# Stage work dealt out by column counts during attention, and one relu moved behind a copy, in a one-layer encoder block

## The chip, the cores and the metric

The kernel runs on one core of a Trainium2 chip. The metric is the device time of one execution in microseconds. TensorE is the matrix engine (PE in the profile), VectorE is DVE, ScalarE is ACT, GpSimd is POOL, and SyncE (SP) issues most of the transfers. Each engine works through its own queue in order; semaphores tie the queues together.

## The reference, cut to what matters

One encoder layer on 1024 tokens of width 1024:

```
u = rms_norm(x, g1)
q, k, v, cb, cc, ch, ga, gb = split(u @ w_in)
y_a = neighbourhood_attention(rms_norm(q), rms_norm(k), v, rpb) @ w_attn_branch   # 8 heads x 64
y_b = (cb * conv3(cc * ch, conv_w)) @ w_conv_branch                               # 512 channels
x = x + (sigmoid(ga) * y_a + sigmoid(gb) * y_b) @ w_o
h = rms_norm(x, g2) @ w_mlp_in                                                    # 4096 wide
x = x + relu(h)^2 @ w_mlp_out
```

The attention window is 8 rows by 16 columns on a 16 x 64 grid, with a learned bias by relative position. Everything is float32 at input and output.

## The kernel before, in words

Each float32 operand is cut into a high and a low 16-bit part, and a product is the sum of three matmuls (`PASSES`). ScalarE makes the high part (a scaled copy), VectorE the low part (scale, then subtract the high part). This holds for weights (`Chunk.prep`, high part L284, low part L276) and for results. Before the parts of a chunk of weights are cut, its scale is found, from sums of squares (ScalarE, L241) or from maxima (VectorE, L295), then a small matmul with a column of ones (L179) and a few VectorE instructions on one column.

The program is written as one stream of issues. Preparations are Python generators in two lists: `fg` holds work that follows from results, `bg` the preparation of weights. `step` and `tick` advance them, and each `yield` in a generator ends what one advance issues. A generator that cannot go on yet yields `WAIT`. So the order on every engine is fixed when the program is built.

**Attention** (about 168 to 327 us). There are 64 steps (4 head pairs, 8 blocks, 2 heads), and a loop of `N + 15` rounds over `k` in which each step's work is spread over 15 rounds: scores (`at_qk`, L785, two matmuls into one of three "s" banks), bias and row maximum on VectorE (`at_max`, L799), exponential on ScalarE (`at_exp`, L808), reciprocals (L812, L813), high part (`at_hi`, ScalarE L821), low part (`at_lo`, VectorE L825), transposition by a transfer on SP (L830), weighted sums of V (`at_pv`, L842), and, when a bank is full, its copy to the high and low part of the result (`at_out`, ScalarE L854 and VectorE L855, in one round). Between these TensorE is given the products of the short convolution (`conv_mms`, L861), seven or eight a round. These need the weights of four convolution chunks; while one chunk is used, the next is prepared from `bg`. When a chunk comes up that is not yet ready, `flush` forces it out.

In the same rounds `conv_step` advances the convolution itself, one chunk at a time: `conv_post` (product of two banks, L687, L691, and the gating product L699), `conv_taps` (the three taps, L705, L708, and GpSimd L710, L713) and `conv_split` (square L720, scale, high part L729, low part L733). The preparation from `bg` gets one `tick` a round, and a second one in rounds in which no parts of weights were cut (`splitting`).

**First MLP product** (about 640 to 930 us). Sixteen groups `q` of columns, each a seven-product scheme (`seven`) on quarter matrices, in `quad`. The seven results are combined through a buffer `AS[q]`, of which there are two, or for the third group (`q == 2`) partly through two spare tiles. ScalarE copies the first bank (L1493), VectorE adds the others (L1474 to L1495). `h_done`, called from `post3` at the end of a group, then does relu (L1439) and square (L1441) on ScalarE, four sums (L1161), and a store to memory (L1452). `post3` of a group runs while the next group's products are already issued. Its arguments `wait1` and `wait2` hold back relu and the sums by so many steps. Meanwhile the weights two groups on are scaled (L954), summed (L963, L968, L934, L935, L179) and cut (L983, L979).

Of the kernel before, what the change touches and what calls it, by code (L numbers as in the profile page):

```python
# [15 lines left out]
OP = mybir.AluOpType  # L16
# [36 lines left out]
def encoder_block(ctx: ExitStack, tc: tile.TileContext, x, weights, cols, gqk, rel, masks, out):  # L53
# [79 lines left out]
    def tick(n=1):  # L133

        for _ in range(n):
            i = 0
            while i < len(bg):
# [5 lines left out]
                else:  # L143
                    break

    def drain():
        while fg:
            step()
# [5 lines left out]
            step()  # L154
        forced[0] = False

    late, units, forced, side, splitting = [], [0], [False], [False], [False]
    work = [0]

    def apart(mark, n=3, of=units):  # L160
# [59 lines left out]
    class Chunk:  # L220
# [9 lines left out]
        def prep(self):  # L230
            n = len(self.widths)
            nk = sum(k for k, _ in self.widths)
            rm, a, b, s = (cols_of("prep", i) for i in (nk, 1, 1, 1))
            self.inv = keep()
            tot = sum(k * w for k, w in self.widths)
            if self.kind in "QKCG" or self.half:
                self.parts = vhome[0][:, 1] if self.half else wsp.tile([128, 2, tot], F16, name="w16_ws", tag="ws")
                for p, (k, w) in enumerate(self.widths):
                    while len(self.raw) <= p:
                        yield WAIT  # L240
                    A.activation(self.parts[:, 1, :k * w].bitcast(BF16), self.raw[p][:, :k * w], AF.Square,  # L241
                                 accum_out=sc[:, at(rm, p)])
                    yield
                V.tensor_reduce(sc[:, a], sc[:, at(rm, 0, n)], axis=AX, op=OP.add)
                c = ones_col()
                V.tensor_tensor(c, sc[:, a], sc[:, gm2], op=OP.mult)
                if not self.half:
                    yield from apart(units[0], 2 if self.kind == "Q" else 3)
                yield from all_sum(c, b, bank(self.bank) if self.bank else anybank(), 1e-36, not self.half)
                yield from pow2_half(b, 14, s, self.inv, more=self.more)  # L250
            else:
                yield from self.largest(rm, a, b)
                yield from pow2(b, 14, s, self.inv, False, more=self.more)
            V.tensor_scalar(sc[:, rm], sc[:, self.rows], sc[:, s], None, op0=OP.mult)  # L254
            yield
            while done[0] < self.first or self.tag not in wpool:
                yield WAIT
            if self.half is not None:
                if not self.half:
                    vhome.append(wsp.tile([128, 2, 2, tot], F16, name="w16_v", tag="ws"))  # L260
                self.parts = vhome[0][:, self.half]
            elif self.kind not in "QKCG":
                self.parts = wpool[self.tag].tile([128, 2, tot], F16, name="w16_" + self.tag, tag=self.tag)
            f = o = 0
            todo = []
            for p, (k, w) in enumerate(self.widths):
                todo.append((p, [(i * w, w, rm.start + o + i) for i in range(k)], f))
                f += k * w
                o += k
            prev = None  # L270
            for it in todo + [None]:
                if prev:
                    p, parts, f = prev
                    for o, m, c in parts:
                        hi, lo = (self.parts[:, w, f + o:f + o + m] for w in range(2))
                        V.scalar_tensor_tensor(lo, self.raw[p][:, o:o + m], sc[:, c:c + 1], hi,  # L276
                                               op0=OP.mult, op1=OP.subtract)
                    done[0] += 1
                    load_upto(done[0] + 5)
                splitting[0] = True  # L280
                if it:
                    p, parts, f = it
                    for o, m, c in parts:
                        A.activation(self.parts[:, 0, f + o:f + o + m], self.raw[p][:, o:o + m], AF.Copy,  # L284
                                     scale=sc[:, c:c + 1])
                prev = it
                self.split = it is None
                yield

        def largest(self, rm, a, b):  # L290
            o = 0
            for p, (k, w) in enumerate(self.widths):
                while len(self.raw) <= p:
                    yield WAIT
                V.tensor_reduce(sc[:, at(rm, o, k)], self.raw[p][:, :k * w].rearrange("p (k w) -> p k w", k=k),  # L295
                                axis=AX, op=OP.max, apply_absolute_value=True)
                o += k
                yield
            while not self.ready:
                yield WAIT  # L300
            mul(rm, self.rows, rm)
            yield
            V.tensor_reduce(sc[:, a], sc[:, rm], axis=AX, op=OP.max, apply_absolute_value=True)
            c = ones_col()
            V.tensor_copy(c, sc[:, a])
            if self.kind != "V":
                yield from apart(units[0], 3 if self.kind != "O" else 1 + (self is cO[1]))
            yield from all_sum(c, b, bank(self.bank) if self.bank else anybank(), 1e-30, self.kind != "V")
# [369 lines left out]
    def conv_post(j, g, half, ps, d):  # L678
# [3 lines left out]
        if g == 0:  # L682
            if half == 0:
                d["z"] = w2p.tile([128, S + 2], F32, name="z", bufs=1)
                G.memset(d["z"][:, 0:1], 0.0)
                G.memset(d["z"][:, S + 1:S + 2], 0.0)
            A.activation(perm(d["z"][:, 1:S + 1], half), p3, AF.Copy, scale=sc[:, ch.inv])  # L687
            return
        if g == 1:
            zn = perm(d["z"][:, 1:S + 1], half)  # L690
            V.tensor_tensor(zn, p3, zn, op=OP.mult)  # L691
            if half == 1:
                d["cv"] = w2p.tile([128, S], F32, name="cv", bufs=1)
                conv_tail.append(conv_taps(ch, d))
            return
        while not d.get("taps"):
            yield
        cv = d["cv"]
        V.tensor_tensor(perm(cv, half), p3, perm(cv, half), op=OP.mult)  # L699
        if half == 1:  # L700
            conv_tail.append(conv_split(j, cv))

    def conv_taps(ch, d):
        z, cv, c = d["z"], d["cv"], ch.cwj
        A.activation(cv, z[:, 0:S], AF.Copy, scale=sc[:, at(c, 0)])  # L705
        yield
        yield
        V.scalar_tensor_tensor(cv, z[:, 1:S + 1], sc[:, at(c, 1)], cv, op0=OP.mult, op1=OP.add)  # L708
        yield
        G.tensor_scalar(z[:, 2:], z[:, 2:], sc[:, at(c, 2)], 1.0, op0=OP.mult, op1=OP.mult)  # L710
        yield
        for c in range(0, S, 256):
            G.tensor_tensor(cv[:, c:c + 256], cv[:, c:c + 256], z[:, c + 2:c + 258], op=OP.add)  # L713
        yield
        d["taps"] = True

    def conv_split(j, cv):
        ch = cConv[j]
        m, s, inv = tmp(), tmp(), tmp()
        A.activation(BT[:, 1, j].bitcast(BF16), cv, AF.Square, accum_out=sc[:, m])  # L720
        yield
        V.tensor_scalar(sc[:, m], sc[:, m], 1e-36, None, op0=OP.max)
        yield
# [1 line left out]
        mul(inv, ch.inv, at(rowsB, j))  # L725
        G.tensor_scalar(cv, cv, sc[:, s], 1.0, op0=OP.mult, op1=OP.mult)
        yield
        bh, bl = (BT[:, w, j].rearrange("p (b r c) -> p b r c", b=8, r=16) for w in range(2))
        A.activation(bh, perm(cv), AF.Copy)  # L729
        yield  # L730
        pv = perm(cv)
        for b in range(0, 8, 2):
# [25 lines left out]
        V.tensor_scalar(sc[:, at(rowsA, k)], sc[:, cV[k // 2].inv], 2.0 ** 20, None, op0=OP.mult)  # L758
    for ch in cA:
        ch.ready = True  # L760

    def conv_step(n):

# [81 lines left out]
        for e in range(2):  # L845
            del st[s + e]

    def at_out(s):
        p, i, _ = steps[s]
        if i % 4 == 3:  # L850
            O = obank[p, i // 4]
            half = slice((i // 4) * 512, (i // 4 + 1) * 512)
            hi, lo_ = QD[:, p, 0, 0, half], QD[:, p, 0, 1, half]
            A.activation(hi, O, AF.Copy, scale=2.0 ** -14)  # L854
            V.scalar_tensor_tensor(lo_, O, 2.0 ** -14, hi, op0=OP.mult, op1=OP.subtract)  # L855

    conv = conv_mms(first)

# [1 line left out]
        for ps, l, r, a, b in islice(conv, n):  # L860
            T.matmul(ps, l, r, start=a, stop=b)  # L861

    for k in range(N + 15):
        p, w = k // 16, k % 16
        if p < 3 and w == 3:
            bias[p + 1] = bias_load(p + 1)
        if p < 3 and w in (9, 11):
            bias_make(*bias[p + 1], (w - 9) // 2)
        ok = lambda d: 0 <= k - d < N
        if ok(0):  # L870
            at_qk(k)
        emit(4)
# [11 lines left out]
            at_exp(k - 1)  # L884
        units[0] += 1
        conv_step(1)
        splitting[0] = False
        tick(1)
        if not splitting[0]:
            tick(1)  # L890
        emit(4 if k % 8 == 0 else 3)
        if k % 2 == 1 and ok(11):
            at_pv(k - 11)
        if k % 2 == 0 and ok(14):
            at_out(k - 14)
    emit(1000)
    while conv_live or conv_tail or conv_q:
        conv_step(1)
    for ch in cB:
        ch.ready = True  # L900
# [560 lines left out]
    def quad(q, c0=0, c1=512):  # L1461
# [24 lines left out]
        def post3(ps):  # L1486
# [1 line left out]
            if q == 0:  # L1488
                fg.append(h_done(q, c0, c1, 3, 4 if c0 else 24))
            elif c1 == 512:  # L1490
                fg.append(h_done(q, 0, c1, *((2, 6) if q == 1 else ())))
        seven(P1[q], actU2, c0, c1, {
            1: lambda ps: A.activation(z[4], ps[1], AF.Copy),  # L1493
            6: post6, 5: None if c0 else post5,
# [262 lines left out]
```

## Time and profile before

| | us |
|---|---|
| median of three executions | 1235.99 |
| lowest, highest | 1235.72, 1236.13 |
| profiled execution, its own time | 1236.98 |
| span of the profiled execution | 1235.0 |

The span is the time from the first to the last instruction on the core; 1.98 us of the profiled execution's time lie around it. In the profile's rows a line number is that of the kernel before. A row of the view of lines names the line, engine, operation, output and inputs, shapes and count, then busy us and the mean ns of one, then idle time ahead of the group and what ended it. A row of the timeline has the start, the time it took, and in square brackets the idle time ahead of it with what ended it. A row of the view of waits has the total in us, the count, and the longest. In a row of the view by stretches the columns are the stretch, its length, the busy time of TensorE, its weight loads, VectorE, ScalarE and GpSimd, then the granted TensorE clock, the share of the transfer engines, and GB/s.

### The profile page before, as it was taken

The numbers are of one execution on the slowest core, as the hardware profiler recorded it, in microseconds if no ns is written. First come the engines' busy times: TensorE is split into PE (matmuls) and PEld (weight loads), VectorE is DVE, ScalarE is ACT, GpSimd is POOL, SyncE is SP. The second block draws the span as 40 slices with busy tenths as digits, with TensorE's granted clock in tenths as the row PEclk, the third lists the DMA queues.
The fourth block names the chain that finished last, engine by engine and source line by source line (L and its number), as shares of the span: only waits on it lengthen the run. The fifth ranks groups of instructions, "written<-read, shape, count | busy, mean of one in ns | idle before, by whom it ended". The sixth has DMA issues, their size and how long they took to land.

```text
span 1235.0 us, 17055 instructions
## 1 busy us (share of the span) xinstructions
PE 1198.7 (97%) x6294; PEld 574.6 (47%) x6294; DVE 932.7 (76%) x1754; ACT 768.2 (62%) x1186; POOL 422.5 (34%) x273
## 2 busy tenths in 40 slices
PE   4999998999999999999999999999999999999998
PEld 3544444444444444444458444444444444444444
DVE  6667877888557686887888664555547999998997
ACT  6785777787464454536668777777765763646430
POOL 0440003112231111101003466655648373463562
PEclk9999999999999999999999999999999999999999
DMA  6548555756561211216096544554484844435202
GB/s 261 117 185 171 109 114 120 154 122 103 131 142 43 68 52 51 69 35 256 18 181 155 193 149 152 169 186 138 146 289 162 307 162 161 175 113 217 102 35 103
DMA packets 170867, 173.35 MB, mean 140 GB/s; under 512 B 131488, under 2 KB 132000, under 8 KB 166688
## 3 DMA queue, kind: packets, MB, share of 16 engines
q1 hardware_dynamic: 170208, 168.07, 46.5%
q10 hardware_dynamic: 576, 4.19, 0.9%
q8 instruction: 49, 0.80, 0.3%
q14 instruction: 34, 0.28, 0.1%
HBM read 102.51 MB, written 37.75 MB: 114 GB/s over the span
## 4 chain that ended last, share of the span: by engine, by line
PE 61%; DVE 22%; ACT 9%; issue 5%; DMA 3%; SPq 0%; ACTq 0%; DVEq 0%
PE ps_d L188 23%; PE ps_s L188 20%; PE ps_o L188 15%; PE ps_d L861 3%; DVE sz L799 2%; DVE P L825 2%; DVE w_s L979 2%; DVE w_ws L276 1%; ACT w_ws L241 1%; DVE ops L1590 1%; DMA qD<-q 1%; DVE w L979 1%; DVE u L416 1%; DVE s L480 1%; DVE sg L1095 1%
## 5 line engine op out<-in xcount | busy, mean ns | idle before, releaser
L188 PEld LDWEIGHTS <-ops 128*128 128x128 f16 x1356 | 132.4, 98 | 159.4 <-issue 2.4
L188 PEld LDWEIGHTS <-w 128*128 128x128 f16 x1368 | 133.2, 98 | 144.7 <-issue 5.9
L861 PE MATMUL ps_d<-uT,w_ws 128*128 128x512 f16 x528 | 125.4, 379 | 0.0
L188 PE MATMUL ps_d<-ops 128*128 128x512 f16 (+1 forms) x528 | 118.3, 374 | 0.0
L188 PE MATMUL ps_s<-ops 128*128 128x512 f16 x492 | 113.2, 379 | 1.6 <-DVE ops L1590 1.1
L1581 ACT ACTIVATE ops<-hf,sc 128x2048 f16<-128x2048 f32 x26 | 52.0, 2000 | 95.3 <-PE ps_o L188 35.9
L188 PEld LDWEIGHTS <-uT 128*128 128x128 f16 x648 | 64.7, 100 | 69.0 <-issue 4.3
L968 POOL TENSOR_TENSOR tsum<-raw 128x512 f32<-128x512 f32 x28 | 45.7, 1646 | 146.0 <-ACT raw L954 146.0
L1161 POOL TENSOR_TENSOR as<-as 128x512 f32<-128x512 f32 x56 | 76.7, 1370 | 44.4 <-ACT as L1441 41.1
L188 PEld LDWEIGHTS <-w_s 128*128 128x128 f16 x588 | 56.7, 98 | 69.5 <-DVE w_s L979 2.0
L188 PE MATMUL ps_d<-u2x,w 128*128 128x512 f16 (+1 forms) x360 | 80.0, 372 | 0.0
L188 PE MATMUL ps_o<-ops 128*128 128x512 f16 x336 | 77.1, 379 | 0.0
L1583 DVE SCALAR_TENSOR_TENSOR ops<-hf,sc,ops 128x2048 f16<-128x2048 f32 x26 | 72.2, 2776 | 5.2 <-ACT ops L1581 5.2
L861 PEld LDWEIGHTS <-w_ws 128*128 128x128 f16 x528 | 50.8, 98 | 52.5
L188 PE MATMUL ps_o<-u2T,w 128*128 128x512 f16 (+1 forms) x324 | 73.4, 377 | 0.0
L954 ACT ACTIVATE raw<-raw,sc 128x256 f32<-128x256 f32 x172 | 71.0, 496 | 1.1 <-DMA raw<-in_weights 1.1
L968 POOL TENSOR_TENSOR gsum<-raw 128x512 f32<-128x512 f32 x14 | 19.0, 1374 | 131.7 <-ACT raw L954 55.3
L983 ACT ACTIVATE w<-raw,sc 128x512 f16<-128x512 f32 (+1 forms) x28 | 24.7, 929 | 49.8 <-DVE sc L404 49.8
L808 ACT ACTIVATE sz<-sz,sc 128x384 f32<-128x384 f32 (+1 forms) x64 | 37.4, 584 | 27.0 <-DVE sc L799 13.7
L1474 DVE TENSOR_TENSOR as<-ps_d,as 128x512 f32<-128x512 f32 (+1 forms) x14 | 9.4, 672 | 58.5 <-ACT as L1493 58.5
L188 PE MATMUL ps_s<-u2T,w 128*128 128x512 f16 (+1 forms) x252 | 52.7, 359 | 0.0
L284 ACT ACTIVATE w_ws<-raw,sc 128x512 f16<-128x512 f32 (+2 forms) x72 | 41.3, 639 | 15.6 <-DVE sc L254 15.6
(339 smaller groups left out, 2624.0 us busy)
## 6 DMA issues: line engine op xcount, KB each, us to landing
raw<-in_weights SPq DMA_DIRECT2D x89, 512.0 KB, 5.8
hs<-as SPq DMA_DIRECT2D x16, 1792.0 KB, 8.7
hf<-hs SPq DMA_DIRECT2D x26, 1024.0 KB, 6.2
w2x<-in_weights SPq DMA_DIRECT2D x16, 512.0 KB, 8.2
raw<-in_weights SPq DMA_DIRECT2D x16, 384.0 KB, 3.6
xt<-in_x SPq DMA_DIRECT2D x8, 512.0 KB, 10.2
gs<-s ACTq DMA_DIRECT2D x4, 1024.0 KB, 4.5
x<-in_x SPq DMA_DIRECT2D x8, 512.0 KB, 10.0
```

The costliest lines, as they stand in the source:

```text
L188: T.matmul(ps, l, r, start=a, stop=b)
L284: A.activation(self.parts[:, 0, f + o:f + o + m], self.raw[p][:, o:o + m], AF.Copy, scale=sc[:, c:c + 1])
L799: V.tensor_tensor_reduce(z[:, :d["n"]], d["ps"][:, :d["n"]], bm, sc[:, cneg], 3.0e38, OP.add, OP.min, accum_out=sc[:, d["mx"]])
L808: A.activation(z, z, AF.Exp, scale=-1.0, bias=sc[:, d["mx"]], accum_out=sc[:, d["sm"]])
L825: V.scalar_tensor_tensor(d["lo"], d["z"][:, :d["n"]], sc[:, d["r"]], d["hi"], op0=OP.mult, op1=OP.subtract)
L861: T.matmul(ps, l, r, start=a, stop=b)
L954: A.activation(v, v, AF.Copy, scale=sc[:, at(g, 4 * i + k)])
L968: G.tensor_tensor(t[:, o], a, b, op=OP.add)
L979: V.scalar_tensor_tensor(o(1), w, sc[:, s], o(0), op0=OP.mult, op1=OP.subtract)
L1161: sub.tensor_tensor(z[o], z[a], z[b], op=op)
L1581: A.activation(P[:, 1, 0], hf, AF.Copy, scale=sc[:, Rs])
L1583: V.scalar_tensor_tensor(P[:, 1, 1], hf, sc[:, Rs], P[:, 1, 0], op0=OP.mult, op1=OP.subtract)
```

## The change

Three things are edited.

- In attention the fixed one or two ticks a round give way to an account of issued work. `debt` holds nanoseconds of VectorE and ScalarE work. Every round takes off 2050 and adds 1200 and 1120 for the softmax; pieces of conv and weight work add amounts worked out from their columns (`spend`). The preparation is advanced up to three times a round, as long as neither engine's account has reached 2250 (`room`, `fill`).
- The copy of a full bank is done in two rounds: high part in the even round, low part in the odd one after it. The loop has one round more. `conv_taps` and `conv_split` yield once more each.
- In the first MLP product `h_done` of the third group gets `wait1 = 2`.

```
+    debt = [0, 0]
+    def spend(v=0, a=0):
+        debt[0] += v
+        debt[1] += a
+    def fill():
+        i = 0
+        while i < len(bg):
+            r = advance(bg[i])
+            if not r:
+                bg.pop(i)
+            elif r != WAIT:
+                return True
+            elif not side[0]:
+                return False
+            else:
+                i += 1
+        return False
...
# Chunk.prep: one square; low parts; high parts. Chunk.largest: one maximum
+                    spend(0, 300 + k * w * 7 // 8)
-                splitting[0] = True
+                    spend(sum(m + 130 for _, m, _ in parts))
+                    spend(0, sum(m * 7 // 8 + 120 for _, m, _ in parts))
+                spend(k * w + 180)
...
# conv_post, conv_taps, conv_split: spend(0, 600), spend(620), spend(620), spend(0, 1020),
# spend(1200), spend(0, 1150), spend(0, 1020) beside the instructions, and one more yield in each of the last two
...
+    SPAN = 2050
+    def room():
+        return max(debt) < SPAN + 200
...
-    def at_out(s):
+    def at_out(s, low):
...
-            A.activation(hi, O, AF.Copy, scale=2.0 ** -14)
-            V.scalar_tensor_tensor(lo_, O, 2.0 ** -14, hi, op0=OP.mult, op1=OP.subtract)
+            if not low:
+                A.activation(hi, O, AF.Copy, scale=2.0 ** -14)
+                spend(0, 550)
+            else:
+                V.scalar_tensor_tensor(lo_, O, 2.0 ** -14, hi, op0=OP.mult, op1=OP.subtract)
+                spend(620)
...
-    for k in range(N + 15):
+    debt[:] = [0, 0]
+    for k in range(N + 16):
...
+            spend(550)
         ok = lambda d: 0 <= k - d < N
+        debt[:] = [max(0, v - SPAN) for v in debt]
+        spend(1200, 1120)
...
         conv_step(1)
-        splitting[0] = False
-        tick(1)
-        if not splitting[0]:
-            tick(1)
+        for _ in range(3):
+            if not room() or not fill():
+                break
...
-        if k % 2 == 0 and ok(14):
-            at_out(k - 14)
+        if ok(14 + k % 2):
+            at_out(k - 14 - k % 2, k % 2)
...
-                fg.append(h_done(q, 0, c1, *((2, 6) if q == 1 else ())))
+                fg.append(h_done(q, 0, c1, *((2, 6) if q == 1 else (2, 0) if q == 2 else ())))
```

More of the change, by code (lines that the diff above doesn't have):

```diff
@@ L155, in flush @@
         forced[0] = False
-    late, units, forced, side, splitting = [], [0], [False], [False], [False]
+    late, units, forced, side = [], [0], [False], [False]
     work = [0]
@@ L687, in conv_post @@
             A.activation(perm(d["z"][:, 1:S + 1], half), p3, AF.Copy, scale=sc[:, ch.inv])
+            spend(0, 600)
             return
@@ L699, in conv_post @@
         V.tensor_tensor(perm(cv, half), p3, perm(cv, half), op=OP.mult)
+        spend(620)
         if half == 1:
@@ L705, in conv_taps @@
         A.activation(cv, z[:, 0:S], AF.Copy, scale=sc[:, at(c, 0)])
+        spend(0, 1020)
         yield
@@ L708, in conv_taps @@
         V.scalar_tensor_tensor(cv, z[:, 1:S + 1], sc[:, at(c, 1)], cv, op0=OP.mult, op1=OP.add)
+        spend(1200)
         yield
@@ L714, in conv_taps @@
         yield
+        yield
         d["taps"] = True
@@ L720, in conv_split @@
         A.activation(BT[:, 1, j].bitcast(BF16), cv, AF.Square, accum_out=sc[:, m])
+        spend(0, 1150)
         yield
@@ L727, in conv_split @@
         yield
+        yield
         bh, bl = (BT[:, w, j].rearrange("p (b r c) -> p b r c", b=8, r=16) for w in range(2))
         A.activation(bh, perm(cv), AF.Copy)
+        spend(0, 1020)
         yield
@@ L853, in at_out @@
             hi, lo_ = QD[:, p, 0, 0, half], QD[:, p, 0, 1, half]
-            A.activation(hi, O, AF.Copy, scale=2.0 ** -14)
-            V.scalar_tensor_tensor(lo_, O, 2.0 ** -14, hi, op0=OP.mult, op1=OP.subtract)
+            if not low:
[3 more added lines that the diff above has]
+                V.scalar_tensor_tensor(lo_, O, 2.0 ** -14, hi, op0=OP.mult, op1=OP.subtract)
+                spend(620)
     conv = conv_mms(first)
@@ L893, in encoder_block @@
             at_pv(k - 11)
-        if k % 2 == 0 and ok(14):
-            at_out(k - 14)
+        if ok(14 + k % 2):
+            at_out(k - 14 - k % 2, k % 2)
     emit(1000)
     while conv_live or conv_tail or conv_q:
+        debt[:] = [0, 0]
         conv_step(1)
```

## The prediction

> **What bounds the kernel now.** I read the page first: the head, and the line of TensorE.
>
> ```profile
> span 1235.0 us, 17055 instructions
> PE 1198.7 (97%) x6294; PEld 574.6 (47%) x6294; DVE 932.7 (76%) x1754; ACT 768.2 (62%) x1186; POOL 422.5 (34%) x273
> ```
>
> TensorE is occupied nearly throughout, so an edit on VectorE or ScalarE pays only where TensorE waits or runs slowly. I therefore went stage by stage to its waits. In attention (170 to 330 us) the view of waits has one entry for it; the chain of waits shows what a step costs when nothing is late; the timeline shows the waits themselves, of which seven of nine stand here (the other two, near 226 and 276 us, are the 0.4 us missing from the sum).
>
> ```profile
> PE ps_s L785 <- DVE sc L799: 7.8, 9, 1.5
> ...
> 300.27 1.51 PE ps_d L861 x7
> 301.78 0.33 PE ps_s L785 x2
> 303.62 0.62 PE ps_o L842 x18
> ...
> 186.87 0.48 PE L785 MATMUL ps_s<-kD,qD 128*128 128x384 f16 x2 [0.64 <-DVE sc L799]
> 189.77 0.48 PE L785 MATMUL ps_s<-kD,qD 128*128 128x384 f16 x2 [0.90 <-DVE sc L799]
> 202.53 0.48 PE L785 MATMUL ps_s<-kD,qD 128*128 128x384 f16 x2 [1.55 <-DVE sc L799]
> 232.34 0.38 PE L785 MATMUL ps_s<-kD,qD 128*128 128x256 f16 x2 [1.24 <-DVE sc L799]
> 251.58 0.48 PE L785 MATMUL ps_s<-kD,qD 128*128 128x384 f16 x2 [1.50 <-DVE sc L799]
> 294.88 0.48 PE L785 MATMUL ps_s<-kD,qD 128*128 128x384 f16 x2 [1.11 <-DVE sc L799]
> 297.39 0.48 PE L785 MATMUL ps_s<-kD,qD 128*128 128x384 f16 x2 [0.48 <-DVE sc L799]
> ```
>
> A step of TensorE (seven conv products, two scores, eighteen weighted sums every second step) takes 1.51 + 0.33 + 0.31 = 2.15 us, 1.84 before the sums begin. The scores have three banks, and L799 frees them: TensorE waits when VectorE falls about two steps behind. The waits add up to 7.8 us. Conv products follow each other every 1.51 / 7 = 0.216 us although each is drawn 0.379 long (first row of the next fence), so every wait hides 0.16 more: 7.8 + 9 x 0.16 = 9.2 us. That is all that attention can return. From 308 us on, when no scores are left, TensorE shows no wait.
>
> These are the instructions that VectorE and ScalarE share out there (view of lines, 170 to 328 us; count, then busy us and mean ns):
>
> ```profile
> L861 PE MATMUL ps_d<-uT,w_ws 128*128 128x512 f16 x504 | 119.7, 379 | 0.0
> L825 DVE SCALAR_TENSOR_TENSOR P<-sz,sc,P 128x384 f16<-128x384 f32 (+1 forms) x64 | 42.7, 669 | 1.4 <-ACT P L821 1.4
> L808 ACT ACTIVATE sz<-sz,sc 128x384 f32<-128x384 f32 (+1 forms) x64 | 37.4, 584 | 27.0 <-DVE sc L799 13.7 <-DVE sc L812 13.2
> L821 ACT ACTIVATE P<-sz,sc 128x384 f16<-128x384 f32 (+1 forms) x64 | 36.8, 576 | 1.6 <-issue 1.3 <-DMA PT<-P 0.3
> L799 DVE CUSTOM_DVE_ANT_0 sz<-ps_s,biasm,sc 128x384 f32<-128x384 f32 x47 | 28.7, 612 | 1.3 <-DVE P L825 0.2
> L276 DVE SCALAR_TENSOR_TENSOR w_ws<-raw,sc,w_ws 128x384 f16<-128x384 f32 (+1 forms) x32 | 17.0, 576 | 0.0
> L284 ACT ACTIVATE w_ws<-raw,sc 128x384 f16<-128x384 f32 (+1 forms) x32 | 16.7, 577 | 0.0
> L241 ACT ACTIVATE w_ws<-raw 128x768 bf16<-128x768 f32 (+1 forms) x10 | 8.8, 879 | 0.2
> L708 DVE SCALAR_TENSOR_TENSOR cv<-z,sc,cv 128x1024 f32<-128x1024 f32 x4 | 5.1, 1278 | 0.0
> L720 ACT ACTIVATE bT<-cv 128x1024 bf16<-128x1024 f32 x4 | 4.2, 1058 | 11.0 <-DVE cv L699 11.0
> ```
>
> The softmax alone costs VectorE 0.61 + 0.67 = 1.28 us a step and ScalarE 0.58 + 0.58 = 1.16. Some 0.9 us a step is free on each; the waits come from steps that get more.
>
> The other place is MLP group 3 (timeline, 696 to 732 us):
>
> ```profile
> 696.02 0.53 SPq L1452 DMA_DIRECT2D hs<-as  x1
> 705.09 0.68 DVE L1487 TENSOR_TENSOR as<-ps_s,as 128x512 f32<-128x512 f32 x1
> 705.80 1.91 ACT L1439 ACTIVATE as<-as 128x2048 f32<-128x2048 f32 x1 [5.68 <-DVE as L1487]
> 707.75 2.00 ACT L1441 ACTIVATE as<-as,sc 128x2048 f32<-128x2048 f32 x1
> 709.75 0.58 ACT L1493 ACTIVATE as<-ps_o 128x512 f32<-128x512 f32 x1
> 710.36 0.69 DVE L1474 TENSOR_TENSOR as<-ps_d,as 128x512 f32<-128x512 f32 x1 [4.59 <-ACT as L1493]
> 711.14 0.16 DVE L935 CAST ones<-sc 128x1 bf16<-128x1 f32 x1
> 711.36 0.16 PE L179 MATMUL ps_s<-ones 128*128 128x1 bf16 x1 [3.36 <-DVE ones L935]
> 711.38 4.44 PE L188 MATMUL ps_o<-u2T,w 128*128 128x512 f16 x12
> 712.75 1.76 ACT L983 ACTIVATE w<-raw,sc 128x512 f16<-128x512 f32 x2 [2.43 <-DVE sc L404]
> 715.65 2.75 PE L188 MATMUL ps_d<-u2x,w 128*128 128x512 f16 x12
> 715.85 0.69 DVE L1495 TENSOR_TENSOR as<-ps_o,as 128x512 f32<-128x512 f32 x1 [3.08 <-PE ps_o L188]
> 730.74 0.16 DVE L935 CAST ones<-sc 128x1 bf16<-128x1 f32 x1
> 731.19 0.17 PE L179 MATMUL ps_s<-ones 128*128 128x1 bf16 x1
> ...
> 712.00:725.00 13.00, 13.00 (x55) 5.61 (x54) 9.78 (x14) 9.23 (x16) 9.00 (x7) 0.88 0.66 218
> ```
>
> Relu and square of the third group (L1439, L1441) run ahead of the copy of the fourth group's first bank (L1493). VectorE has L1474 at the head of its queue, waiting for that copy, and behind it L935, for which TensorE waits at L179. After the wait the granted clock is 0.88 over 712 to 725 us and twelve products take 4.44 us instead of 2.75.
>
> **MLP group.** Nothing is added; two ScalarE instructions move behind one. In the built order the copy stands directly ahead of relu and square. TensorE's wait, 3.36 + 0.16 hidden, and the slow products, 4.44 - 2.75 = 1.69, are 5.2 us. The copy needs the buffer of the second group, which is stored from 696.02 on:
>
> ```profile
> hs<-as SPq DMA_DIRECT2D x16, 1792.0 KB, 8.7
> ```
>
> It lands at about 704.7, the copy ends at 705.3, and relu, queued behind, cannot begin before 705.78 in any case: cost nothing, by 0.5 us. L1474 then follows L1487 at 705.8 and L935 ends near 706.9, before TensorE arrives (711.36 - 3.52 = 707.8). Relu and square end when they did, so the third group's own store does not move.
>
> What is late next is the fourth group's sum at L179: 0.29 us in hand before (730.90 against 731.19), and TensorE now comes 5.2 us sooner. The weights between them start with L983, which follows the square at 709.85 instead of starting at 712.75: 2.9 sooner. If that were all, 5.2 - 2.9 - 0.3 = 2.0 us of wait would stay. But L979 stands behind L1495, which waited for the slow products, and that goes too, so nearly all of the 5.2 may carry: 0. I take 0.6, nearer to the second, since L979 is on the path: gain 4.6 (bounds 3.2 and 5.2).
>
> [...]
>
> **Attention.** No instruction is added or removed; the counts per engine are the same in the built order. What moves is the step in which the stages' pieces are issued, and L855 comes one step after L854. I put the pieces of the built order on their steps, at the mean times above:
> - 186 to 190 us, two waits, 1.9 with the hidden part. Before: two L276 (1.15) in each of four successive steps, with L708 in one: 2.43 to 3.71 against TensorE's 1.84. Now they stand in steps 4, 5, 7 and 10. But step 4 gives ScalarE four L284 at once, 4 x 0.577 = 2.3 us ahead of an L821 for which L825 waits. The burst changes engine: I keep all 1.9.
> - 202.53, 1.7. Before: L720 and four L241 in two ScalarE steps, 1.06 + 3.52 + 2.32 = 6.9 against 4.3. Now two L241, then L720, then one L241 in each of two later steps: 1.16 + 1.76 and 1.16 + 1.06, 5.1 against 4.3. I keep 0.3.
> - 226 to 232, two waits, 1.8. The second is VectorE held at L855:
>
> ```profile
> 231.07 0.69 DVE L855 SCALAR_TENSOR_TENSOR qD<-ps_o,qD 128x512 f16<-128x512 f32 x1 [1.80 <-ACT qD L854]
> ```
>
>   A step later L854 is done. But L708 and L855 now meet in step 28, 1.28 + 1.28 + 0.69 = 3.25. I keep 0.8.
> - 251.58, 1.7: paired L241, then again L854 ahead of L855. Both are spread: 0.2.
> - The last three waits (0.2 near 276 us, then 1.11 and 0.48; 2.2 with the hidden part) come from two L276 in four steps running, and from L720 with two L241 in one: 0.6. Steps 47 to 51 now carry the fourth chunk at VectorE's full pace: 0.3 new.
>
> That keeps 1.9 + 0.3 + 0.8 + 0.2 + 0.6 + 0.3 = 4.1 of 9.2: gain 5.1. Bounds: 9.2 if every wait goes; below, -6 (the slow rival). The pieces must still be early: the third chunk's last L276 stands in step 31, and TensorE reaches those columns in step 36, five steps of 2.15 us later; the fourth chunk's in 51 against 56. Extra yields, and the one more round of the loop, issue nothing by themselves. The loads and transposes on SP hang on the same steps and move with them.
>
> **Sum.** The profiled execution took 1236.98 us, 0.99 over the median. 1236.98 - 5.1 - 4.6 = 1227.3; on the median's scale 1226.3.
>
> **Rivals.**
> - Only the MLP part pays. ScalarE's bursts (step 4 above) reach TensorE through L821 and L825 as the old ones did, so attention returns nothing: 1235.99 - 4.6 = 1231.4. For it: ScalarE has steps of 1.16 + 2.3 = 3.5 us in the built order. Against: VectorE's longest runs are broken up.
> - The MLP wait moves to the fourth group: 2.0 us stay there and the clock drops again (1.69), so 1.5 of the 5.2 is gained; with attention 1235.99 - 5.1 - 1.5 = 1229.4. For it: 0.29 us in hand. Against: the products ahead run at full rate.
> - Slower. By my count the built order has thirteen steps with over 2.5 us on VectorE or 2.7 on ScalarE. If each costs TensorE 1.2 us (the mean of the old waits is 9.2 / 9 = 1.0), that is 15.6 instead of 9.2, 6.4 lost; with 4.6 gained 1237.8. It decides once a burst exceeds the two steps that three banks hold. Against: the old order has 23 such steps and only nine waits.
>
> **How the numbers follow.** Forecast 0.60, only MLP 0.18, moved MLP wait 0.11, slower 0.11. Around the forecast I go 4 us down (9.2 instead of 5.1 in attention) and far enough up for the first two rivals: 1222.0 to 1234.0, with the slower case and a little of both edges left out. Under 0.2% (2.5 us) cannot be told from no change. Faster 0.83 (the three gains less a margin), same 0.06, slower 0.11.
>
> **What will show it.** Right: no wait of TensorE at the third group's L179, twelve products there in 2.75 us, granted clock 1.00; TensorE's waits on L799 about 4 us instead of 7.8, none behind L855; the first conv-only stretch begins near 303 instead of 308 us. Wrong: a wait of over 1.5 us at the fourth group's L179, waits on L799 of 7 us or more, or a time over 1234.

## The result, and the profile after

The changed kernel took 1226.88 us (median of six executions, 1226.16 to 1227.98) beside 1236.82 us for the kernel before in the same series. The ratio is 0.9921, with a 95% interval of 0.9908 to 0.9933: about 9.8 us faster. The forecast was 1226.3 us, in a range of 1222 to 1234. Run once more beside other kernels, it gave 0.9928 (0.9915 to 0.9940).

Line numbers in the rows below are those of each kernel itself. In the changed kernel the scores are L824 (L785 before), the row maximum L838 (L799), the conv products L904 (L861), the bank copy L894 and L897 (L854, L855), the small matmul with ones L201 (L179), its column L982 (L935), the cutting of MLP weights L1030 and L1026 (L983, L979), the sums on GpSimd L1208 (L1161), relu and square L1486 and L1488 (L1439, L1441), the copy of a group's first bank L1540 (L1493), the first result on VectorE L1521 (L1474), the store L1499 (L1452).

The page of the changed kernel:

```profile
span 1224.1 us, 17058 instructions
PE 1195.7 (98%) x6294; PEld 572.6 (47%) x6294; DVE 935.4 (76%) x1754; ACT 766.2 (63%) x1186; POOL 425.9 (35%) x273
```

Every engine executes as many instructions as before. TensorE is busy 3.0 us less, slow products among it, and the span is 10.9 us shorter, so most of what went is time between instructions. The view of waits of TensorE, over the same 170 to 330 us as before (us, times, longest):

```profile
PE ps_s L824 <- DVE sc L838: 2.4, 4, 1.2
```

These four in its timeline, each wait in brackets:

```profile
183.09 0.49 PE L824 MATMUL ps_s<-kD,qD 128*128 128x384 f16 x2 [0.66 <-DVE sc L838]
185.82 0.49 PE L824 MATMUL ps_s<-kD,qD 128*128 128x384 f16 x2 [0.28 <-DVE sc L838]
188.08 0.48 PE L824 MATMUL ps_s<-kD,qD 128*128 128x384 f16 x2 [0.26 <-DVE sc L838]
191.91 0.38 PE L824 MATMUL ps_s<-kD,qD 128*128 128x256 f16 x2 [1.21 <-DVE sc L838]
```

Of nine waits with 7.8 us, four with 2.4 are left, all before 192 us. With the 0.16 us that each hides, 9.2 became 2.4 + 4 x 0.16 = 3.0. The ends of the stage, before and then after, are its first score and the first product of the gate stage:

```profile
162.54 0.38 PE L785 MATMUL ps_s<-kD,qD 128*128 128x256 f16 x2
327.41 0.82 PE L188 MATMUL ps_s<-uT,w_ws 128*128 128x512 f16 x3
```

```profile
160.99 0.38 PE L824 MATMUL ps_s<-kD,qD 128*128 128x256 f16 x2
319.83 1.47 PE L210 MATMUL ps_s<-uT,w_ws 128*128 128x512 f16 x6
```

Attention fell from 164.87 to 158.84 us: 6.0 us. It began 1.5 us sooner in this execution; the work ahead of it is the same in both kernels, and over the runs below its start lies between 160.6 and 162.5 us, so that 1.5 us is no part of the change. It more than covers the 1.0 us by which the spans differ beyond the medians (10.9 against 9.9 us).

The MLP groups, in the timeline of the changed kernel:

```profile
697.16 0.60 ACT L1540 ACTIVATE as<-ps_o 128x512 f32<-128x512 f32 x1 [4.78 <-DMA hs<-as]
698.08 1.91 ACT L1486 ACTIVATE as<-as 128x2048 f32<-128x2048 f32 x1 [0.33 <-DVE as L1534]
698.74 0.16 DVE L982 CAST ones<-sc 128x1 bf16<-128x1 f32 x1
700.10 0.17 PE L201 MATMUL ps_s<-ones 128*128 128x1 bf16 x1
700.13 2.75 PE L210 MATMUL ps_o<-u2T,w 128*128 128x512 f16 x12
702.19 6.51 POOL L1208 TENSOR_TENSOR as<-as 128x512 f32<-128x512 f32 x4 [5.54 <-ACT as L1488]
703.53 4.05 DVE L1026 SCALAR_TENSOR_TENSOR w<-raw,sc,w 128x512 f16<-128x512 f32 x2
708.73 0.53 SPq L1499 DMA_DIRECT2D hs<-as  x1
718.51 0.57 ACT L1540 ACTIVATE as<-ps_o 128x512 f32<-128x512 f32 x1
719.90 0.16 DVE L982 CAST ones<-sc 128x1 bf16<-128x1 f32 x1
720.11 0.16 PE L201 MATMUL ps_s<-ones 128*128 128x1 bf16 x1 [1.69 <-DVE ones L982]
```

The copy waits for the store of the second group, as foreseen, and is through before relu could begin. TensorE comes to L201 at 700.10 without a wait, and the twelve products after it take 2.75 us. One group on, at 720.11, it waits 1.69 us where it had 0.29 us in hand before.

### The profile page after: what moved, and what is told of

The parts are those of the page before. It is cut to its first block, busy times and chain, and to the rows that moved or that the text cites. A ratio compares the mean times of both kernels' runs of the same rounds, so it can differ in the third digit from the quotient of the medians.

```text
span 1224.1 us, 17058 instructions
## 1 busy us (share of the span) xinstructions
PE 1195.7 (98%) x6294; PEld 572.6 (47%) x6294; DVE 935.4 (76%) x1754; ACT 766.2 (63%) x1186; POOL 425.9 (35%) x273
## 4 chain that ended last, share of the span: by engine, by line
PE 67%; DVE 18%; ACT 8%; issue 4%; DMA 3%; SPq 0%; ACTq 0%; DVEq 0%
PE ps_d L210 22%; PE ps_s L210 19%; PE ps_o L210 15%; PE ps_d L904 8%; DVE ops L1637 2%; DVE w_s L1026 2%; PE ps_o L881 1%; PE ps_s L824 1%; DMA qD<-q 1%; DVE w L1026 1%; DVE w_ws L299 1%; DVE u L441 1%; DVE s L505 1%; ACT w_ws L263 1%; DVE sg L1142 1%
## 5 line engine op out<-in xcount | busy, mean ns | idle before, releaser
L904 PE MATMUL ps_d<-uT,w_ws 128*128 128x512 f16 x528 | 125.4, 379 | 0.0
L1208 POOL TENSOR_TENSOR as<-as 128x512 f32<-128x512 f32 x56 | 77.8, 1389 | 43.1 <-ACT as L1488 39.9
L904 PEld LDWEIGHTS <-w_ws 128*128 128x128 f16 x528 | 50.8, 98 | 52.6
L1030 ACT ACTIVATE w<-raw,sc 128x512 f16<-128x512 f32 (+1 forms) x28 | 24.6, 926 | 46.4 <-DVE sc L429 46.4
L1521 DVE TENSOR_TENSOR as<-ps_d,as 128x512 f32<-128x512 f32 (+1 forms) x14 | 9.4, 671 | 53.8 <-ACT as L1540 53.8
```

The costliest lines, as they stand in the source:

```text
L1030: A.activation(o(0), w, AF.Copy, scale=sc[:, s])
L1208: sub.tensor_tensor(z[o], z[a], z[b], op=op)
```

## The experiments

For each kernel two kinds of stretch are read from its timeline: attention (first score to first gate product), and the time from one L179 to the next in the MLP, first across the third group's wait (689.67 to 711.36 us before), then the next two. Without a wait or slow products an MLP group takes 18.15 us. A row of the table holds for one profiled execution.

```
kernel            attention   MLP: third   fourth   fifth
before              164.87       21.69     19.83    18.16
changed             158.84       18.15     20.01    18.15
mlp_only            164.83       18.15     20.02    18.15
att_only            158.88       21.68     18.16    18.15
account_only        159.36       21.68     18.15    18.16
banks_only          159.31       21.68     21.11    18.16
no_limit            168.99       21.69     19.63    18.15
early_one           157.86       18.16     20.03    18.15
relu_two            158.85       18.16     18.89    20.89
sums_v_relu_two     158.91       23.39     20.07    18.16
banks_mlp           159.34       18.15     20.02    18.15
best_w6             157.85       18.15     18.16    19.65
```

### The MLP part alone

```
 # kernel before
-                fg.append(h_done(q, 0, c1, *((2, 6) if q == 1 else ())))
+                fg.append(h_done(q, 0, c1, *((2, 6) if q == 1 else (2, 0) if q == 2 else ())))
```

> The kernel before with the third group's relu behind the copy, nothing else. Theory: the two parts of the change are independent, and this one gives what the trace of the changed kernel shows at the third and fourth group, 5.2 us less a new wait of 1.85 at the fourth group: about 3.4 us faster, 0.997 of before; no wait of TensorE at the third group's L179, a wait of 1.5 to 2 us at the fourth's. Rival (the slow clock after the wait was something else): the wait goes but twelve products still take 4.4 us, 1.7 us faster.

Measured: 0.9975 (0.9965 to 0.9984), 3.1 us. In the trace the third group's wait is gone and the fourth's is 1.7 us, as in the changed kernel; the three stretches sum to 56.32 us instead of 59.68, 3.4 us less. The theory held.

### Attention alone

```
 # changed kernel
-                fg.append(h_done(q, 0, c1, *((2, 6) if q == 1 else (2, 0) if q == 2 else ())))
+                fg.append(h_done(q, 0, c1, *((2, 6) if q == 1 else ())))
```

> The changed kernel with the third group's relu back ahead of the copy. Theory: attention from its first score to the first gate product 6.0 us shorter than before (158.8 against 164.9 us), the MLP wait of 3.4 us with 4.4 us for twelve products back: about 6 us faster, 0.995. Rival (attention's gain is taken back by the gate stage): the first gate product comes 6 us sooner but the MLP's first group less than 4 us sooner, 3 us faster in all.

Measured: 0.9948 (0.9937 to 0.9960), 6.4 us. Attention is 6.0 us shorter, and from the first gate product to the third group's first L179 both kernels take 362.3 us: the gate stage takes nothing back. The rival fell. The MLP wait is back, but not the slow products that the theory put behind it (timeline):

```profile
704.57 0.16 PE L201 MATMUL ps_s<-ones 128*128 128x1 bf16 x1 [3.37 <-DVE ones L982]
704.60 2.75 PE L210 MATMUL ps_o<-u2T,w 128*128 128x512 f16 x12
```

The view by stretches over those products (each engine's busy time, GpSimd's, then granted clock):

```profile
704.00:708.00 4.00, 3.43 (x17) 1.58 (x17) 2.44 (x12) 2.03 (x3) 3.76 (x4) 1.00 0.01 4
```

The same wait of 3.37 us is followed by products at full rate, and the granted clock stays 1.00 (the column after GpSimd's). So in its profiled execution this kernel lost 1.69 us less in the MLP than the kernel before, though the order of its MLP is the same.

### The account without the two-step copy, and the two-step copy without the account

```
 # account_only: changed kernel, relu as before
-        if ok(14 + k % 2):
-            at_out(k - 14 - k % 2, k % 2)
+        if k % 2 == 0 and ok(14):
+            at_out(k - 14)          # both halves, spend(620, 550)
```

> The changed attention with both halves of a bank's copy in one round again, and the relu as before. Theory (the account spreads the pieces, the two-step copy removes the holds at L855): VectorE waits 1 to 2 us at the low half of some banks again, and two or three of TensorE's waits of about 1 us come back, so attention is 2 us longer than with the two-step copy, 4 us faster than before. Rival (with the pieces spread, ScalarE reaches the high half in time anyway): within 0.5 us of the kernel with both attention edits.

```
 # banks_only: kernel before
-    for k in range(N + 15):
+    for k in range(N + 16):
...
-        if k % 2 == 0 and ok(14):
-            at_out(k - 14)
+        if ok(14 + k % 2):
+            at_out(k - 14 - k % 2, k % 2)
 # at_out split into a high and a low half as in the change, without spend
```

> The kernel before with the two-step copy of banks alone (one more round of the loop, no account). Theory: only the waits that directly follow a hold at L855 go (two of nine, 1.24 and 1.50 us): 1 to 2.5 us faster. Rival (the bursts set the waits, and the hold only falls on the same place): under 0.5 us.

Measured: 0.9957 (0.9943 to 0.9971) and 0.9960 (0.9948 to 0.9972). Both theories fell: by the traces the account alone shortens attention by 5.5 us, the two-step copy alone by 5.6, and the two together by 6.0. The rival of the first came in its number (0.5 us longer than with both edits), but not for its reason: in the kernel with the account alone VectorE is still held at the low half, yet TensorE hardly notices. The rival of the second fell too. The view of waits over the stage, VectorE's, then TensorE's:

```profile
DVE qD L894 <- ACT qD L893: 5.7, 3, 2.9
```

```profile
PE ps_s L824 <- DVE sc L838: 2.8, 5, 1.2
```

One of the five, 0.35 us, stands after 205 us. With the two-step copy alone every piece of the preparation stands where it stood, and three waits are left, all before 205 us, at the places and of the sizes that they had. The view of waits, then the timeline:

```profile
PE ps_s L785 <- DVE sc L799: 3.1, 3, 1.5
```

```profile
185.50 0.48 PE L785 MATMUL ps_s<-kD,qD 128*128 128x384 f16 x2 [0.64 <-DVE sc L799]
188.40 0.48 PE L785 MATMUL ps_s<-kD,qD 128*128 128x384 f16 x2 [0.90 <-DVE sc L799]
201.14 0.48 PE L785 MATMUL ps_s<-kD,qD 128*128 128x384 f16 x2 [1.53 <-DVE sc L799]
```

VectorE's holds at the low half, in the kernel before and then here, went from five to one:

```profile
DVE qD L855 <- ACT qD L854: 7.1, 5, 2.2
```

```profile
DVE qD L857 <- ACT qD L855: 0.7, 1, 0.7
```

So the waits after 205 us needed both the old places of the pieces and the holds at L855, and taking away either is enough (but for the 0.35 us). For those waits the two edits are not terms of a sum. That a hold uses up the lead of the three banks, which the full steps behind it don't give back, is the reading of this; some of the waits stand about ten us or more behind the nearest hold, and no run followed the lead from the one to the other.

### No limit

```
 # changed kernel, relu as before
-            if not room() or not fill():
+            if not fill():
```

> The changed attention with no limit from the account: three advances of the preparation in every round, whatever has been issued; two-step copy kept, the relu as before. Theory (either edit alone leaves enough in hand, since the two-step copy alone took away every wait after 205 us): bursts three pieces long return, but attention stays within 2 us of the 158.9 us with both edits. Rival (the two-step copy only suffices with at most two ticks a round, and it is the account that bounds a burst): waits on L799's counterpart of 6 us or more, attention 162 us or longer.

Measured: 1.0030 (1.0018 to 1.0043), slower than before. Attention takes 168.99 us. The theory fell and the rival held: with three advances in every round the two-step copy does not suffice. The view of waits, TensorE's, then VectorE's:

```profile
PE ps_s L824 <- DVE sc L838: 9.9, 9, 2.5
```

```profile
DVE sc L267 <- ACT w_ws L263: 11.2, 3, 4.4
```

Squares of a chunk (L263, L241 before) now stand up to three in a row on ScalarE, and VectorE is held at the sum that follows them (L267) three times. The first hold, of 3.26 us, ends at 200.31, and TensorE's longest wait follows it. The longest, of 4.43 us near 248 us, is followed by no wait of TensorE until 266 us. The timeline of TensorE behind the first:

```profile
201.11 0.38 PE L824 MATMUL ps_s<-kD,qD 128*128 128x256 f16 x2 [2.48 <-DVE sc L838]
202.41 1.44 PE L904 MATMUL ps_d<-uT,w_ws 128*128 128x512 f16 x3
203.78 1.17 PE L881 MATMUL ps_o<-PT,vT 128*64 128x128 f16 x18
```

Not all of the loss is waiting. Three products take 1.44 us here and 0.81 elsewhere, and the eighteen weighted sums behind them 1.17 where those at 208.92 us take 0.69. With what each wait hides, the waits are 11.3 us against 9.2 before, 2.1 us more; attention is 4.1 us longer, and the slow stretch stands for most of the rest.

### One advance a round at first

```
 # changed kernel
-        for _ in range(3):
+        for _ in range(1 if k < 12 else 3):
```

> The changed kernel with at most one advance of the preparation a round in the first twelve rounds. Theory (the waits left at 182 to 192 us come from four high copies in one step on ScalarE, ahead of the softmax's high part): no step has four, the waits fall from 3.0 to under 1.5 us, attention 157.5 us, 1.5 us faster than the changed kernel. Rival (there is simply more VectorE work before step 12 than TensorE's pace of 1.84 us a step allows): the waits move but stay near 3 us.

Measured: 0.9916 (0.9902 to 0.9929); attention 157.86 us, 1.0 us shorter than in the changed kernel.

```profile
PE ps_d L904 <- DVE w_ws L299: 0.3, 1, 0.3
```

```profile
186.80 4.69 DVE L299 SCALAR_TENSOR_TENSOR w_ws<-raw,sc,w_ws 128x384 f16<-128x384 f32 x8
192.21 0.38 PE L824 MATMUL ps_s<-kD,qD 128*128 128x256 f16 x2 [1.30 <-DVE sc L838]
```

The waits near 183 to 188 us are gone, but this doesn't show that they came from the four high copies. The edit moved VectorE's work too: of the eight low parts, six stood ahead of 182 us in the changed kernel, and here all eight come at once from 186.80 on, just before the products that read them, so that TensorE waits 0.3 us for the columns themselves. The wait of 1.30 us follows these eight, so it is a new one, not the one of 1.21 us that stood near 192 us. And in the trace of the changed kernel the four high copies hold VectorE only once, for 0.61 us (view of waits of VectorE, 170 to 193 us, then the view by stretches):

```profile
DVE w_ws L299 <- ACT w_ws L308: 0.6, 1, 0.6
```

```profile
183.00:193.00 10.00, 8.16 (x64) 4.10 (x64) 9.93 (x22) 5.31 (x14) 5.98 (x9) 1.00 0.54 114
```

VectorE is busy for 9.93 of these 10 us. That speaks for the rival, too much VectorE work for TensorE's pace: the waits moved, though they fell from 2.4 to 1.6 us in the view of waits. By time the kernel can't be told from the changed one (0.9921).

### The fourth group's relu behind the copy too

```
 # changed kernel
-  (2, 0) if q == 2 else ()
+  (2, 0) if q in (2, 3) else ()
```

> The changed kernel with the fourth group's relu behind the fifth group's copy too. Theory (the copy must wait for the store of the third group, which lands 8.6 us after 708.7, so the copy ends at about 718 instead of 719.1, and the relu behind it starts 3.4 us later): the wait at the fourth group's L179 falls from 1.7 to about 0.7 us, but the fourth group's relu, square and store come 3 to 4 us later and a wait of similar size appears one group on: within 1 us of the changed kernel. Rival (the later relu is hidden): 1 us faster.

Measured: 0.9949 (0.9936 to 0.9963), about 3 us slower than the changed kernel. Timeline:

```profile
717.94 0.60 ACT L1540 ACTIVATE as<-ps_o 128x512 f32<-128x512 f32 x1 [6.10 <-DMA hs<-as]
719.57 0.16 PE L201 MATMUL ps_s<-ones 128*128 128x1 bf16 x1 [0.57 <-DVE ones L982]
740.46 0.16 PE L201 MATMUL ps_s<-ones 128*128 128x1 bf16 x1 [2.58 <-DVE ones L982]
740.48 4.24 PE L210 MATMUL ps_o<-u2T,w 128*128 128x512 f16 x12
```

Here the copy does wait for a store (6.10 us), relu is queued behind it, and the wait of 0.57 us is as foreseen. But the wait one group on is 2.58 us, not of similar size, and it was followed by slow products, 4.24 instead of 2.75 us. The mechanism was right, its price too small.

### The third group's sums on VectorE

```
 # relu_two
-        if q > 1:
+        if q > 2:
             yield from sums(v, G)
```

> As the run before, and the third group's four sums on VectorE instead of GpSimd. Theory (GpSimd's sums, 6.5 us beside VectorE's low parts, made the two L979 of 512-wide rows take 4.05 instead of 1.94 us and held the store back): the low parts are back to about 2 us, the store of the third group starts 3 us sooner, so the copy is free at about 715 and the wait at the fourth group's L179 is gone: 1.5 to 2 us faster than the changed kernel. Rival (2.8 us of sums on VectorE cost what the low parts gain): the wait stays at 1 us or more.

Measured: 0.9970 (0.9959 to 0.9982), about 6 us slower than the changed kernel where the theory had it 1.5 to 2 us faster. The place of the sums was wrong: on VectorE they stand ahead of L982 and wait there for the square.

```profile
702.73 2.87 DVE L1208 TENSOR_TENSOR as<-as 128x512 f32<-128x512 f32 x4 [3.50 <-ACT as L1488]
705.91 0.16 PE L201 MATMUL ps_s<-ones 128*128 128x1 bf16 x1 [5.07 <-DVE ones L982]
711.25 1.94 DVE L1026 SCALAR_TENSOR_TENSOR w<-raw,sc,w 128x512 f16<-128x512 f32 x2
```

One part of the theory stands nonetheless. The first two low parts (one of 512 columns, one of 1024; the row merges them) take 1.94 us with GpSimd idle but for the last 0.4 us, against 4.05 in the changed kernel beside GpSimd's sums.

### The two-step copy and the MLP part, without the account

```
 # banks_only
-                fg.append(h_done(q, 0, c1, *((2, 6) if q == 1 else ())))
+                fg.append(h_done(q, 0, c1, *((2, 6) if q == 1 else (2, 0) if q == 2 else ())))
```

> The kernel before with the two-step copy and the third group's relu behind the copy, no account. Theory (the two attention edits take away the same waits): attention 159.3 us against the changed kernel's 158.8, the time within 1 us of the changed kernel, ratio 0.992 to 0.993. Rival (the account gives something of its own, beyond the waits): 2 us or more slower than the changed kernel.

> The changed kernel itself, beside the next two on one chip. Theory: 0.992 of before, as measured; 1.69 us of wait at the fourth group's L179.

Measured on one chip: 0.9932 (0.9918 to 0.9945) without the account, 0.9928 (0.9915 to 0.9940) with it. The theory held: attention is 159.34 us, 0.5 us longer than with the account, and by time the two kernels can't be told apart. Two small edits give the whole gain that can be measured.

### A version with less waiting

```
 # early_one
-                ... (2, 0) if q == 2 else ()
+                ... (2, 6) if q == 2 else (2, 0) if q == 3 else ()
...
-        if q > 1:
+        if q > 2:
             yield from sums(v, G)
```

> The changed kernel with one advance a round in the first twelve rounds, the third group's sums on VectorE behind its L1542's counterpart (the fifth result of the fourth group) instead of on GpSimd, and the fourth group's relu behind the fifth group's copy. Theory: the low parts of 512-wide rows take about 2 us again instead of 4.05, the third group's store starts near 706 instead of 708.7, the copy is free at about 715, and the wait at the fourth group's L179 is gone; with 1 us less in attention about 2.7 us faster than the changed kernel, ratio 0.990. Rival (the 2.9 us of sums on VectorE push the low parts back as far as they gain, or the later relu costs a wait one group on as before): no faster than with one advance alone, 0.9915.

Measured: 0.9910 (0.9896 to 0.9923), 1224.69 us beside 1227.07 us for the changed kernel on the same chip.

```profile
702.70 2.86 DVE L1208 TENSOR_TENSOR as<-as 128x512 f32<-128x512 f32 x4
705.48 1.94 DVE L1026 SCALAR_TENSOR_TENSOR w<-raw,sc,w 128x512 f16<-128x512 f32 x2
705.67 0.53 SPq L1499 DMA_DIRECT2D hs<-as  x1
714.57 0.60 ACT L1540 ACTIVATE as<-ps_o 128x512 f32<-128x512 f32 x1 [4.11 <-DMA hs<-as]
717.43 0.17 PE L201 MATMUL ps_s<-ones 128*128 128x1 bf16 x1
737.08 0.16 PE L201 MATMUL ps_s<-ones 128*128 128x1 bf16 x1 [1.33 <-DVE ones L982]
```

The low parts, the store and the copy came as the theory said, and the fourth group's wait is gone. But the shorter low parts did not do it: behind the sums on VectorE, the next additions of the fourth group (L1529 onward) start 12.5 us after the third group's L201, against 11.8 in the changed kernel. What helped is relu behind the copy, with a store early enough for that. The rival's wait one group on came in part: 1.33 us at the fifth group's L201, and that group takes 19.65 us instead of 18.15. So the MLP part gains 0.4 us by the trace and attention 1.0; the other 1.0 us between the two medians lies, by the two traces, ahead of attention and behind the fifth group's L201, so that it is no effect that the theory names. It has the lowest median of all kernels here, but its interval overlaps that of the changed kernel.

## Why the prediction was right, point by point

- **The bound.** That TensorE's waits behind L799 and the one MLP wait are where this change could gain is borne out: the rest of the trace runs alike (362.3 us from the first gate product to the third group's first L179 before and in att_only, 362.1 in the changed kernel; 485.7 and 485.8 us from the fifth group's L179 to the end).
- **Attention, 5.1 of 9.2 us.** Measured: 6.0 in the trace, 6.4 by the runs of attention alone. That the total came near is in part luck, since two errors of the ledger offset each other. At the first place I kept 1.9 us for the burst that moves to ScalarE, and 3.0 stayed; that this burst is the cause is not shown, since it held VectorE for 0.61 us and early_one moved VectorE's low parts with it. Everything kept at the other places, 2.2 us, did not stay.
- **The causes at those places.** I gave each wait one cause, a burst here and a hold at L855 there. That step was wrong: after 205 us each needed both. The 2.2 us of waits from 276 us on, which I put down to bursts alone, go with the two-step copy alone (banks_only). Undoing one edit alone, as banks_mlp does, looks as if that edit did nothing.
- **The MLP, 4.6 us.** Measured: 3.4 in the trace, 3.1 by the runs of that part alone. The mechanism held step by step: the copy waits for the store at no cost, the third group's wait goes, the next to be late is the fourth group's L179. One term was mis-sized. The wait left there I put at 0.6 us between bounds of 0 and 2.0; it is 1.69 + 0.16 = 1.85. I had reckoned that L979 would move up with L1495, and it did, but into the time of GpSimd's sums, where its first two instructions take 4.05 instead of 1.94 us. These 2.1 us stand on the way to the late copy and are more than the 1.85; that they alone make the wait is worked out from the rows, and no run took them away alone. Another term has no fixed size: the 1.69 us of slow products came after a wait of 3.36 us, and after waits of 3.36 and 3.37 us account_only and att_only lost none.
- **The sum.** 5.1 + 4.6 = 9.7 forecast, 9.8 by the ratio; attention was 0.9 too low, the MLP 1.2 too high. That these two nearly cancel is luck.
- **The signs.** Those named for being right came: no wait at the third group's L201, products at full rate, four waits behind L838 with 2.4 us where I had about 4, and the first conv-only stretch at 300.8 us, which is 302.3 with attention's start as before, where I had 303. But one sign of being wrong came as well: the wait at the fourth group's L201, 1.69 us, is over the 1.5 that I had set.
- **The rivals.** The first did not come. The second came by half: the MLP wait did move to the fourth group, at nearly the 2.0 us that the rival gave it, but the clock did not drop after it (granted 1.00 over 718 to 731 us), and so 3.4 instead of 1.5 us were gained. The slow rival's mechanism is real, and the account is what keeps it off in this change: without the limit the time is 0.3% over that of before, a part of it by slow products after one wait of 2.48 us. The thirteen full steps that I counted in the built order left four waits.

## What to carry to other kernels

A wait that needs two causes goes away with either, so edits tried one at a time look equally good and their gains don't add; undo each from the full change as well as trying it alone before one of them is kept as the cause. When a stall is moved forward in time, look at what its successors will then run beside: here two instructions of a chain that was set free early ran beside another engine's sums and took 4.05 us instead of 1.94. Count the slowness of the clock after a stall as a chance, not as a price: behind waits of 3.36 and 3.37 us it cost between nothing and 2.95 us here.

## What the runs showed of the hardware

The clock after a wait. The same wait for L179 or its counterpart cost differently from one execution to the next. In the kernel with the two-step copy alone (timeline, then the view by stretches):

```profile
704.36 0.16 PE L179 MATMUL ps_s<-ones 128*128 128x1 bf16 x1 [3.36 <-DVE ones L937]
704.39 5.28 PE L188 MATMUL ps_o<-u2T,w 128*128 128x512 f16 x12
```

```profile
703.00:710.00 7.00, 5.64 (x15) 2.05 (x15) 2.54 (x11) 4.58 (x7) 4.99 (x4) 0.54 0.09 33
```

Here 3.36 us of waiting cost 2.95 us more (a group of 21.11 instead of 18.16; granted clock 0.54 over 703 to 710 us), before the change 1.69, in att_only and account_only nothing (granted clock 1.00 over 704 to 708 us in both). Shorter waits were followed by slow products too, 2.58 us in relu_two (twelve in 4.24 instead of 2.75 us) and 2.48 us in attention without the limit (three in 1.44 instead of 0.81 us), while those of 1.69 to 1.71 us in the changed kernel, mlp_only, early_one and banks_mlp were not (the group behind took 18.15 us in each). No run was made to shift a wait, and what it takes for the clock to fall stays open.

VectorE beside GpSimd. The same two low parts took 1.94 us with GpSimd nearly idle and 4.05 us beside its sums, and GpSimd's four sums took 6.51 us there. In the kernel before, they took 1.2 us less (timeline):

```profile
709.92 5.31 POOL L1161 TENSOR_TENSOR as<-as 128x512 f32<-128x512 f32 x4 [5.54 <-ACT as L1441]
```

So the low parts and the sums each took longer beside the other; what makes them slow is not shown.

In attention the times go the same way. In the changed kernel a low part of the softmax, at 185.69, took 1.27 instead of 0.61 us while GpSimd was at the third tap (L740), and two low parts of weights, at 189.42, took 1.90 instead of 1.14 us while it was at L743. The ledger goes by mean times (0.67 us, and 1.15 for two) and the account by columns, so these steps were fuller than either says. Whether that makes the waits left from 185.8 to 191.9 us was not tried.
